# Logsumexp over heads on one core: one more head summed by ScalarE, 80 bias columns moved from GpSimd to VectorE, four more tiles in 4 MB loads

## The chip, the cores and the metric

The kernel runs on one core of a Trainium2 chip. The metric is the device time of one execution in microseconds (us), the median of the runs shown. A profile comes from one profiled execution; its span runs from the first to the last recorded event on the core.

## The reference

```python
B, S, D, H = 8, 2048, 2048, 8          # x: (B, S, D) float32, bias: (H, D // H)
x_heads = x.reshape(B, S, H, Dh).transpose(0, 2, 1, 3)      # Dh = 256
x_heads = x_heads + bias[None, :, None, :]
x_tiled = np.repeat(x_heads, 2, axis=2)
mx = x_tiled.max(axis=-1, keepdims=True)
lse = mx.squeeze(-1) + np.log(np.exp(x_tiled - mx).sum(axis=-1))   # (B, H, 2 * S)
```

For each row of x and each of its eight heads: add the head's 256 biases, take the exponentials, sum them, take the logarithm, and write the result twice. x has 134 MB and is read once; the output has 1 MB. The kernel sums exponentials without taking the maximum off first, watches for sums out of the usual range, and has a second way for that case (`all_again`), which does not run here.

## The kernel before, in words

**Tiles.** A tile t is 256 rows of x: 128 partitions with K = 2 rows each, 2 MB. There are 64 tiles, eight to a batch. SBUF holds eight tiles at a time, as four 4 MB buffers `xb` of two tiles each. `load` (L228, L243) issues all loads of x on SyncE's (SP's) queue: tiles 0 and 1 by themselves, then from tile 2 up to `BLOCKS` - 1 in blocks of 4 MB for two tiles, then tile by tile (2 MB), from tile 57 on by single rows (1 MB), and the last three tiles in an order written out by hand (`TAIL_LOADS`, 1 MB down to 128 KB). A load into a buffer waits until the last readers of the tiles that were in it are done (`last_uses`); `reload` issues it right after the work of the tile that frees it. SP also issues the stores of the results, behind all loads. Each DMA reports to one of eight semaphores in turn, and a DMA waits for the earlier DMA that reported to the same one.

**Three stages** (`STAGES`). Tiles 0 to 53 use `BULK`, called whole tiles below; tiles 54 to 56 use `MIXED`; from tile 57 on rows are done singly, and from tile 61 on the steps follow a list written out by hand (`TAIL`).

**A whole tile** divides its eight heads between engines by the numbers in `BULK`:

- Heads 0 to 2 (`pe=3`): TensorE puts the bias into PSUM (`put_bias`, L370) and adds x to it (`late_heads`, L428). Head 0 lies in the bank `one_ps`, heads 1 and 2 in one of two pairs of banks, `pair`, which alternate. ScalarE takes the exponentials. For head 0 it sums them on the way, once for each of the two rows (`acc=1`, L439: an activation and a read of its accumulator); for heads 1 and 2 it only writes them back to `xb`, 1024 elements in one instruction (L446).
- Head 3 (columns 768 to 1023): ScalarE takes the exponential of x without a bias, and VectorE multiplies by the exponential of the bias, which lies in the PSUM tile `w_ps` (L496).
- Heads 4 to 7 (from `g0=4`, columns 1024 to 2047): GpSimd adds the bias in place (`g_add`, L478), then ScalarE takes the exponential, in the same instruction as that of head 3 (L484, 2560 elements).
- VectorE sums the exponentials of heads 1 to 7, 3584 elements into 14 sums (L503).

The steps L484, L496 and L503 of a tile stand in `later`, which the program issues in the next tile's turn. `MIXED` tiles do without VectorE's late product over head 3: there GpSimd adds the bias to heads 4 to 7, ScalarE sums two heads, and VectorE multiplies and sums two heads (`weigh`, L519).

**Order.** The order of all instructions on each engine is the order in which the program issues them (`manual_schedule`); nothing moves them later.

**At the start**, ScalarE's queue fetches the bias into `brow` (L280). GpSimd splits the first three heads' bias into three bf16 parts (L293 to L297), which ScalarE's queue copies into `b3` (L298); the first two tiles use the parts directly. TensorE spreads the bias over the partitions (L303) for `b_rep` and `w_ps`.

**At the end of a batch**, its sums are turned by TensorE and logged by ScalarE. For batch 6 (tiles 48 to 55) `turn_two` (L713) does the one after tile 59, and `finish_two` (L726) the other after tile 60.

Of the kernel before, what the change touches and what calls it, by code (L numbers as in the profile page):

```python
# [12 lines left out]
ACT = mybir.ActivationFunctionType  # L13
# [3 lines left out]

K = 2
KB = 4
BLOCKS = 42  # L20

NBUF = 8

# [7 lines left out]

BULK = dict(pe=3, acc=1, g0=4, late=True, fold=0)
MIXED = dict(pe=2, acc=2, g0=4, late=False, fold=0)
PROMPT_F1 = dict(pe=2, acc=2, g0=8, late=False, fold=1)
FOLD = 32
# [55 lines left out]
def kernel(  # L93
# [6 lines left out]
    nc = tc.nc  # L100
    P = nc.NUM_PARTITIONS
    B, S, D = x.shape
    H, Dh = bias.shape
# [4 lines left out]
    T = B * NBLK  # L108
# [3 lines left out]
    CPE = BULK["pe"] * Dh  # L112
    MM = 512
# [9 lines left out]
    brow = sb.tile([1, D], F32, name="brow")  # L123
# [5 lines left out]
    b3 = sb.tile([P, CPE], BF16, name="b3")  # L129
    bparts = sb.tile([1, 3, CPE], BF16, name="bparts")  # L130
# [38 lines left out]
    xts = [xb[:, k : k + K] for xb in xbs for k in range(0, KB, K)]  # L169
# [49 lines left out]
    last_uses = [[] for _ in range(T)]  # L219
# [51 lines left out]
    for set_idx, (_name, funcs) in enumerate(get_activation_tables(nc.m.arch).items()):  # L271
        if ACT.Exp in funcs and ACT.Ln in funcs:
# [4 lines left out]
                )  # L277
            )
            break
    nc.scalar.dma_start(  # L280
        out=brow.rearrange("p (h j) -> p h j", h=H), in_=bias.unsqueeze(0)
    )
    for t in range(NBUF):
        load(t)
    nc.vector.memset(ones, 1.0)
# [9 lines left out]
    nc.gpsimd.tensor_copy(bparts[:, 1], brest[:, 0])  # L295
    nc.gpsimd.tensor_sub(brest[:, 1], brest[:, 0], bparts[:, 1])
    nc.gpsimd.tensor_copy(bparts[:, 2], brest[:, 1])  # L297
    nc.scalar.dma_start(out=b3[0:3, :], in_=bparts)  # L298

# [5 lines left out]
    for i, c in enumerate(range(G0, D, MM)):  # L307
        spread(ps[i], c, c + MM)
        nc.vector.tensor_copy(b_rep[:, c - G0 : c - G0 + MM], ps[i])
    W_LATE = BULK["g0"] * Dh  # L310
    w_late = w_ps[:, 0 : W_LATE - W0]
    spread(w_late, W0, W_LATE)
    nc.scalar.activation(out=w_late, in_=w_late, func=ACT.Exp)
# [109 lines left out]
    def late_heads(m, t, got, sums):  # L423


        mms = []
        for h, p in enumerate(got[:-1]):
            mm = nc.tensor.matmul(  # L428
                p,
                lhsT=ident,  # L430
                rhs=xts[t % NBUF][:, :, h * Dh : (h + 1) * Dh],
                start=False,
                stop=True,
            )
            mms.append(on_x(t, mm, [loads[t, 0, 0]]))

        def pe_part():
            for k in range(K):
                act = nc.scalar.activation(  # L439
                    out=xts[t % NBUF][:, k, 0:Dh],  # L440
                    in_=got[0][:, k * Dh : (k + 1) * Dh],
                    func=ACT.Exp,
                    accum_out=sums[:, k, 0:1],
                )
                last_uses[t].append(on_x(t, act, [mms[0]]))
            act = nc.scalar.activation(  # L446
                out=xts[t % NBUF][:, :, Dh : m["pe"] * Dh].rearrange(
                    "p k (h j) -> p h k j", j=Dh
                ),
                in_=got[-1].rearrange("p (h k j) -> p h k j", k=K, j=Dh),  # L450
                func=ACT.Exp,
            )
            on_x(t, act, [mms[-1]])

        return pe_part
# [17 lines left out]
        )  # L473

    def g_add(m, t, k0, k1):
        c = m["g0"] * Dh
        v = xts[t % NBUF][:, k0:k1, c:D]
        add = nc.gpsimd.tensor_tensor(  # L478
            out=v, in0=v, in1=each_row(b_rep, c - G0, D - c, k1 - k0), op=ALU.add
        )  # L480
        return on_x(t, add, [loads[t, k0, 0]])
# [4 lines left out]
    def later(m, t, k0, k1, sums, add):  # L486
# [2 lines left out]
        v = xts[t % NBUF][:, k0:k1, h0 * Dh : D]  # L489
        done = exp_inplace(t, v, add)  # L490
        if m["late"]:
            n = (m["g0"] - h0) * Dh
            f = v[:, :, 0:n]
            h0 = m["acc"]
            v = xts[t % NBUF][:, k0:k1, h0 * Dh : D]
            mul = nc.vector.tensor_tensor(  # L496
                out=f,
                in0=f,
                in1=each_row(w_ps, m["pe"] * Dh - W0, n, k1 - k0),
                op=ALU.mult,  # L500
            )
            done = on_x(t, mul, [done])
# [356 lines left out]
    for t in range(T_TAIL):  # L859
# [71 lines left out]
        for i, (_, b1) in enumerate(groups):  # L931
            if t - 2 == b1 * NBLK - 1:
                finish(i)
                ends_of(i)
        if t == T - 5:
            turn_two()
        if t == T - 4:
            finish_two()
    store()
    last_bank = heads[0][2]  # L940
# [57 lines left out]
```

## Time and profile before

| what | us |
|---|---|
| median of 3 runs | 322.7 (322.33 to 323.44) |
| the profiled execution | 322.41 |
| its span | 320.5 |
| VectorE busy | 286.8 |
| GpSimd busy | 287.2 |
| ScalarE busy | 264.0 |
| TensorE busy | 248.8 |

In the profile, PE is TensorE, PEld its weight loads, DVE is VectorE, ACT is ScalarE, POOL is GpSimd, SP is SyncE. L12 is line 12 of the kernel. A row of a group of instructions has line, engine, operation, output and input tiles with partitions x elements, the count, busy time and mean duration in ns, and then the engine's idle time before them with what ended it. A row by stretches of the span has for each engine its busy time and count, then TensorE's granted clock (1.00 is full), the mean busy share of the 16 DMA engines (a packet is booked at one moment, so single stretches can go over 1) and the GB/s that they moved. Records on one engine overlap a little, so the distance from one start to the next is shorter than a duration.

### The profile page before, as it was taken

How to read it: one execution, taken by the hardware profiler on the slowest of the kernel's cores; microseconds unless marked ns; L12 is line 12 of the kernel's file. 1: busy time of each engine (PE TensorE's matmuls, PEld its weight loads, DVE VectorE, ACT ScalarE, POOL GpSimd, SP SyncE). 2: the span in 40 equal slices, each digit the busy share in tenths (PEclk: the TensorE clock that was granted, in tenths of full speed). 3: DMA queues.
4: the chain of work that ended last, by engine and by line, in shares of the span. 5: the costliest groups of instructions: out<-in, count | busy, mean ns of one | idle time of the engine just before them, and what ended most of it. 6: DMA issues, size and time to landing. Idle time of an engine off the chain costs nothing.

```text
span 320.5 us, 2268 instructions
## 1 busy us (share of the span) xinstructions
PE 248.8 (78%) x610; PEld 99.1 (31%) x610; DVE 286.8 (89%) x307; ACT 264.0 (82%) x434; POOL 287.2 (90%) x118
## 2 busy tenths in 40 slices
PE   5998884877887877869788776688877787678873
PEld 2333331323333323323233322233332332233321
DVE  2347999799969999996999999989999999999995
ACT  1159977888599788878979988879888998999996
POOL 7939997999999999999999989999999999987864
PEclk9979998999598999968989999989999999799999
DMA  7999999999999999999999999999999999999995
GB/s 310 444 425 458 413 439 436 413 454 405 450 450 401 451 423 429 454 405 447 450 406 454 417 431 454 401 431 431 433 433 425 428 431 430 421 429 427 422 415 224
DMA packets 8950, 135.44 MB, mean 423 GB/s; under 512 B 996, under 2 KB 1383, under 8 KB 2791
## 3 DMA queue, kind: packets, MB, share of 16 engines
q1 hardware_dynamic: 8784, 135.14, 98.6%
q10 hardware_dynamic: 152, 0.14, 0.1%
q8 instruction: 5, 0.08, 0.1%
q14 instruction: 9, 0.07, 0.1%
HBM read 134.23 MB, written 1.05 MB: 422 GB/s over the span
## 4 chain that ended last, share of the span: by engine, by line
DMA 49%; ACT 20%; DVE 13%; PE 13%; POOL 4%; issue 0%; SPq 0%
DMA xb<-in_x_dram 48%; ACT xb L484 12%; DVE R L503 11%; PE pair L428 6%; POOL xb L478 4%; PE one_ps L428 3%; ACT xb L459 3%; ACT xb L446 3%; DVE xb L496 2%; PE pair L303 1%; PE pair L370 1%; ACT xb L439 1%; PE one_ps L370 1%; DMA brow<-in_bias_dram 1%; ACT xb L832 0%
## 5 line engine op out<-in xcount | busy, mean ns | idle before, releaser
L478 POOL TENSOR_TENSOR xb<-xb,b_rep 128x2048 f32<-128x2048 f32 x57 | 257.6, 4542 | 19.5 <-DMA xb<-in_x_dram 19.5
L503 DVE TENSOR_REDUCE R<-xb 128x14 f32<-128x3584 f32 (+1 forms) x57 | 216.8, 3803 | 2.1 <-ACT xb L484 0.2
L484 ACT ACTIVATE xb<-xb 128x2560 f32<-128x2560 f32 (+5 forms) x78 | 155.9, 2008 | 17.6 <-POOL xb L478 17.6
L428 PE MATMUL pair<-xb,ident 128*128 128x512 f32 x216 | 111.9, 644 | 0.0
L428 PE MATMUL one_ps<-xb,ident 128*128 128x512 f32 x108 | 62.9, 666 | 17.1 <-DMA xb<-in_x_dram 17.1
L446 ACT ACTIVATE xb<-pair 128x1024 f32<-128x1024 f32 x54 | 55.5, 1028 | 19.8 <-PE pair L428 19.5
L428 PEld LDWEIGHTS pair<-xb,ident 128*128 128x128 f32 x216 | 45.3, 210 | 59.4 <-issue 59.4
L496 DVE TENSOR_TENSOR xb<-xb,w_ps 128x512 f32<-128x512 f32 x54 | 36.7, 680 | 22.0 <-ACT xb L484 22.0
L370 PE MATMUL one_ps<-b,ones_bf 128*128 128x512 bf16 x52 | 20.1, 387 | 36.7 <-ACT xb L439 36.7
L439 ACT ACTIVATE xb<-one_ps 128x256 f32<-128x256 f32 x108 | 39.9, 378 | 6.6 <-PE one_ps L428 6.4
L370 PEld LDWEIGHTS <-ones_bf 128*128 128x128 bf16 (+1 forms) x174 | 17.6, 101 | 85.7 <-issue 78.8
L370 PE MATMUL pair<-b,ones_bf 128*128 128x512 bf16 x104 | 31.1, 380 | 0.0
L428 PEld LDWEIGHTS one_ps<-xb,ident 128*128 128x128 f32 x108 | 19.5, 198 | 32.2 <-DMA xb<-in_x_dram 26.1
L519 DVE CUSTOM_DVE_ANT_0 xb<-xb,w_ps 128x256 f32<-128x256 f32 x61 | 22.3, 418 | 0.1
L439 ACT ACTIVATION_READ_ACCUMULATOR xb<-one_ps 128x1 f32 x108 | 22.1, 205 | 0.0
L405 PE MATMUL pair<-xb,ident 128*128 128x512 f32 x28 | 16.5, 692 | 6.8 <-DMA xb<-in_x_dram 6.8
L542 POOL TENSOR_TENSOR xb<-xb 128x128 f32<-128x128 f32 (+3 forms) x39 | 15.2, 389 | 4.8 <-ACT xb L832 2.0
L459 ACT ACTIVATE xb<-pair 128x256 f32<-128x256 f32 x37 | 14.0, 397 | 0.1
L821 PE MATMUL pair<-xb,ident 128*128 128x512 f32 (+1 forms) x18 | 8.1, 533 | 3.5 <-DMA xb<-in_x_dram 3.4
L536 POOL TENSOR_TENSOR xb<-xb,w_sb 128x256 f32<-128x256 f32 (+1 forms) x10 | 7.8, 783 | 3.1 <-ACT xb L484 2.6
L405 PEld LDWEIGHTS pair<-xb,ident 128*128 128x128 f32 x28 | 4.9, 207 | 14.9 <-DMA xb<-in_x_dram 12.9
L459 ACT ACTIVATION_READ_ACCUMULATOR xb<-pair 128x1 f32 x37 | 8.3, 224 | 0.0
(61 smaller groups left out, 83.2 us busy)
## 6 DMA issues: line engine op xcount, KB each, us to landing
xb<-in_x_dram SPq DMA_DIRECT2D x20, 4096.0 KB, 21.6
xb<-in_x_dram SPq DMA_DIRECT2D x17, 2048.0 KB, 22.2
xb<-in_x_dram SPq DMA_DIRECT2D x10, 1024.0 KB, 22.0
xb<-in_x_dram SPq DMA_DIRECT2D x2, 640.0 KB, 16.2
xb<-in_x_dram SPq DMA_DIRECT2D x4, 256.0 KB, 8.7
xb<-in_x_dram SPq DMA_DIRECT2D x1, 768.0 KB
xb<-in_x_dram SPq DMA_DIRECT2D x2, 384.0 KB, 13.0
out_dram<-res SPq DMA_DIRECT2D x1, 512.0 KB, 5.8
```

The source lines that it names most:

```text
L370: nc.tensor.matmul(p, lhsT=lhsT, rhs=each_row(b, h * Dh, Dh, K), start=i == 0, stop=False,)
L405: mm = nc.tensor.matmul(p, lhsT=ident, rhs=xts[t % NBUF][:, ka:kb, c : c + w], start=False, stop=True,)
L428: mm = nc.tensor.matmul(p, lhsT=ident, rhs=xts[t % NBUF][:, :, h * Dh : (h + 1) * Dh], start=False, stop=True,)
L439: act = nc.scalar.activation(out=xts[t % NBUF][:, k, 0:Dh], in_=got[0][:, k * Dh : (k + 1) * Dh], func=ACT.Exp, accum_out=sums[:, k, 0:1],)
L446: act = nc.scalar.activation(out=xts[t % NBUF][:, :, Dh : m["pe"] * Dh].rearrange("p k (h j) -> p h k j", j=Dh), in_=got[-1].rearrange("p ...
L459: act = nc.scalar.activation(out=xts[t % NBUF][:, k, h * Dh : (h + 1) * Dh], in_=p, func=ACT.Exp, accum_out=sums[:, k, h : h + 1],)
L478: add = nc.gpsimd.tensor_tensor(out=v, in0=v, in1=each_row(b_rep, c - G0, D - c, k1 - k0), op=ALU.add)
L484: return on_x(t, nc.scalar.activation(out=v, in_=v, func=ACT.Exp), [after])
L496: mul = nc.vector.tensor_tensor(out=f, in0=f, in1=each_row(w_ps, m["pe"] * Dh - W0, n, k1 - k0), op=ALU.mult,)
L503: red = nc.vector.tensor_reduce(out=sums[:, k0:k1, h0:H], in_=v.rearrange("p k (h j) -> p k h j", j=Dh), op=ALU.add, axis=mybir.AxisListTy ...
L519: ttr = nc.vector.tensor_tensor_reduce(out=v, in0=v, in1=w, scale=1.0, scalar=0.0, op0=ALU.mult, op1=ALU.add, accum_out=dst,)
L542: done = nc.gpsimd.tensor_tensor(out=v[:, :, 0:n], in0=v[:, :, 0:n], in1=v[:, :, n : 2 * n], op=ALU.add)
```

## The change

Whole tiles are divided otherwise: `acc=2`, so ScalarE sums heads 0 and 1 itself, in four activations, and writes head 2 back with an activation of 512 elements; VectorE's product takes `MORE = 80` columns beyond head 3, GpSimd's addition starts 80 columns later, and VectorE's sum covers heads 2 to 7, 3072 elements. `w_ps` is filled 80 columns further at the start. `BLOCKS` goes from 42 to 46, so tiles 42 to 45 come in two loads of 4 MB instead of four of 2 MB. The bias and its parts are each fetched in two DMAs. The turning and the logarithm of batch 6 come after tiles 57 and 58. With the two DMAs more at the start the semaphores of the DMAs fall otherwise; the fourth 4 MB load then waits for the first load of all.

```diff
-BLOCKS = 42
+BLOCKS = 46
-BULK = dict(pe=3, acc=1, g0=4, late=True, fold=0)
+BULK = dict(pe=3, acc=2, g0=4, late=True, fold=0)
+
+MORE = 80
...
-    nc.scalar.dma_start(
-        out=brow.rearrange("p (h j) -> p h j", h=H), in_=bias.unsqueeze(0)
-    )
+    for h in range(0, H, H // 2):
+        nc.scalar.dma_start(
+            out=brow.rearrange("p (h j) -> p h j", h=H)[:, h : h + H // 2],
+            in_=bias[h : h + H // 2].unsqueeze(0),
+        )
...
-    nc.scalar.dma_start(out=b3[0:3, :], in_=bparts)
+    for c0, c1 in ((0, MM), (MM, CPE)):
+        nc.scalar.dma_start(out=b3[0:3, c0:c1], in_=bparts[:, :, c0:c1])
...
-    W_LATE = BULK["g0"] * Dh
+    W_LATE = BULK["g0"] * Dh + MORE
...
         def pe_part():
-            for k in range(K):
-                act = nc.scalar.activation(
-                    out=xts[t % NBUF][:, k, 0:Dh],
-                    in_=got[0][:, k * Dh : (k + 1) * Dh],
-                    func=ACT.Exp,
-                    accum_out=sums[:, k, 0:1],
-                )
-                last_uses[t].append(on_x(t, act, [mms[0]]))
+            for h in range(m["acc"]):
+                for k in range(K):
+                    act = nc.scalar.activation(
+                        out=xts[t % NBUF][:, k, h * Dh : (h + 1) * Dh],
+                        in_=got[h][:, k * Dh : (k + 1) * Dh],
+                        func=ACT.Exp,
+                        accum_out=sums[:, k, h : h + 1],
+                    )
+                    last_uses[t].append(on_x(t, act, [mms[h]]))
+            h = m["acc"]
             act = nc.scalar.activation(
-                out=xts[t % NBUF][:, :, Dh : m["pe"] * Dh].rearrange(
-                    "p k (h j) -> p h k j", j=Dh
-                ),
-                in_=got[-1].rearrange("p (h k j) -> p h k j", k=K, j=Dh),
+                out=xts[t % NBUF][:, :, h * Dh : m["pe"] * Dh],
+                in_=got[h].rearrange("p (k j) -> p k j", j=Dh),
                 func=ACT.Exp,
             )
...
     def g_add(m, t, k0, k1):
-        c = m["g0"] * Dh
+        c = m["g0"] * Dh + (MORE if m["late"] else 0)
...
         if m["late"]:
-            n = (m["g0"] - h0) * Dh
+            n = (m["g0"] - h0) * Dh + MORE
...
-        if t == T - 5:
+        if t == T - 7:
             turn_two()
-        if t == T - 4:
+        if t == T - 6:
             finish_two()
```

## The prediction

> **What bounds the kernel now.** I read the page from the top: busy shares first, then the DMA queue, then the load stream by stage.
>
> ```profile
> span 320.5 us, 2268 instructions
> PE 248.8 (78%) x610; PEld 99.1 (31%) x610; DVE 286.8 (89%) x307; ACT 264.0 (82%) x434; POOL 287.2 (90%) x118
> ...
> q1 hardware_dynamic: 8784, 135.14, 98.6%
> ```
>
> Two engines stand at 90%, but the queue of loads stands at 98.6% of the span. An average can hide a starved stage, so the next view is the busy time by stretches of the span; its last two columns are the DMA share and the GB/s.
>
> ```profile
> 60.00:100.00 40.00, 31.84 (x77) 12.45 (x76) 36.12 (x17) 34.15 (x54) 37.47 (x9) 0.91 1.00 433
> 204.00:240.00 36.00, 27.41 (x70) 11.47 (x69) 34.56 (x17) 31.14 (x49) 35.40 (x9) 0.95 0.99 425
> 240.00:270.00 30.00, 23.04 (x63) 9.39 (x62) 29.79 (x15) 27.62 (x43) 30.00 (x7) 1.00 1.01 430
> 300.00:310.00 10.00, 7.70 (x23) 3.14 (x22) 9.96 (x61) 10.00 (x26) 6.93 (x16) 1.00 1.01 419
> ```
>
> The DMA share is full in every stage, whichever engine is busiest beside it: the loads follow each other without a hole. The chain of work that ended last, in order of time, says how far the engines are from opening one (start, duration, what):
>
> ```profile
> 31.60 21.45 DMA xb<-in_x_dram
> ...
> 148.91 0.73 ACT xb L439 x4
> 149.64 0.91 ACT xb L446
> 150.55 2.23 ACT xb L484
> ...
> 187.32 20.63 DMA xb<-in_x_dram
> ...
> 224.73 0.60 DVE xb L496
> ...
> 251.88 24.21 DMA xb<-in_x_dram
> ...
> 283.60 1.45 ACT xb L459 x8
> ...
> 304.83 0.48 ACT xb L832
> ```
>
> The load issued at 31.60 is that of tiles 8 and 9 (four 4 MB buffers hold tiles 0 to 7) and lands at 53.05. The one at 187.32 is the last 4 MB load, tiles 40 and 41, and lands at 207.95. They are 16 loads apart: (207.95 - 53.05) / 16 = 9.681 us each, **4.841 us a tile**. The load at 251.88 follows VectorE's sum of tile 47, so it is tile 55; it lands at 276.09, 14 tiles of 2 MB after 207.95: **4.867 us a tile**. A 4 MB load that needs 9.68 us lands 21.45 or 20.63 us after its issue, so about 11 us of other loads stand ahead of it. An engine may release a buffer 11 us later than now before the queue runs dry. That is the cover for nearly everything below.
>
> The end of the span is tied to the same stream:
>
> ```profile
> 300.80 1.13 PE L405 MATMUL pair<-xb,ident 128*128 128x512 f32 x2 [0.44 <-DMA xb<-in_x_dram]
> ...
> 305.68 1.13 PE L821 MATMUL pair<-xb,ident 128*128 128x512 f32 x2 [0.46 <-DMA xb<-in_x_dram]
> ```
>
> ```profile
> 315.69 0.30 PEld L821 LDWEIGHTS pair<-xb,ident 128*128 128x128 f32 x2 [0.67 <-DMA xb<-in_x_dram]
> ```
>
> ```profile
> 302.88 0.58 ACT L726 ACTIVATE res_two<-pair 64x512 f32<-64x512 f32 x1
> 303.36 1.48 ACT L484 ACTIVATE xb<-xb 128x1536 f32<-128x1536 f32 x1
> ...
> 305.65 1.48 ACT L484 ACTIVATE xb<-xb 128x1536 f32<-128x1536 f32 x1
> ...
> 316.57 0.38 ACT L459 ACTIVATE xb<-pair 128x256 f32<-128x256 f32 x1
> ```
>
> TensorE still waits for data at 305.68 and at 315.69. ScalarE has no gap in the tail, but its exponential at 305.65 starts just as the data that TensorE waited for comes in; and its last sum at 316.57 can't be much earlier, since the last matmul, started at 315.69, ends near 316.4. From the last landing to the end of the span it is 320.5 - 315.7 = 4.8 us, and the change touches none of it.
>
> **The change part by part.** The rows that price it, from the groups with shapes kept apart:
>
> ```profile
> L478 POOL TENSOR_TENSOR xb<-xb,b_rep 128x2048 f32<-128x2048 f32 x57 | 257.6, 4542 | 19.5 <-DMA xb<-in_x_dram 19.5
> L503 DVE TENSOR_REDUCE R<-xb 128x14 f32<-128x3584 f32 x54 | 209.9, 3888 | 1.9
> L428 PE MATMUL one_ps<-xb,ident 128*128 128x512 f32 x108 | 62.9, 666 | 17.1 <-DMA xb<-in_x_dram 17.1
> L439 ACT ACTIVATE xb<-one_ps 128x256 f32<-128x256 f32 x108 | 39.9, 378 | 6.6 <-PE one_ps L428 6.4
> L496 DVE TENSOR_TENSOR xb<-xb,w_ps 128x512 f32<-128x512 f32 x54 | 36.7, 680 | 22.0 <-ACT xb L484 22.0
> L439 ACT ACTIVATION_READ_ACCUMULATOR xb<-one_ps 128x1 f32 x108 | 22.1, 205 | 0.0
> L503 DVE TENSOR_REDUCE R<-xb 128x8 f32<-128x2048 f32 x3 | 6.9, 2284 | 0.2 <-ACT xb L484 0.2
> L484 ACT ACTIVATE xb<-xb 128x2048 f32<-128x2048 f32 x3 | 5.8, 1920 | 0.2 <-POOL xb L478 0.2
> ```
>
> *ScalarE, 54 whole tiles.* Before, back to back: two summed heads 0.73, the exponential of 1024 0.91, that of 2560 2.23, together 3.87 us. After: four summed exponentials (eight records, four of them accumulator reads, take 1.45 in the chain row at 283.60), one of 512 elements (0.48, row at 304.83) and 2.23: **4.16 us**, 0.29 more. If neither reads nor starts overlapped it would be 4 x (0.378 + 0.205) + 0.58 (512 elements, row at 302.88) + 2.23 = 5.14. I take 4.16, since the chain shows four of them in a row. It lies under the 4.84 us between tiles.
>
> *VectorE.* The sum shrinks from 3584 to 3072 elements; by (3888 - 2284) / 1536 = 1.04 ns an element that is 0.53 less. The product grows from 512 to 672: 0.17 more. Start to start 4.51 (0.60, 3.89 and the gaps) becomes about **4.15 us**.
>
> *GpSimd.* 1888 instead of 2048 elements. In proportion, 4.54 becomes 4.19. At worst nothing is saved.
>
> So all three stand under 4.84 a tile, before and after. In the bulk that buys a buffer released about 1 us sooner, a longer queue, and no time: the stream is the limit. **0 us**; if GpSimd or VectorE grew instead, the 11 us would cover it.
>
> *4 MB loads for tiles 42 to 45.* Two loads fewer on SP, and four tiles at 4.841 instead of 4.867: **-0.1 us**. The lower end is the whole shortfall of the stretch 204 to 240, 36 x (433 - 425) / 433 = -0.7; the upper end is 0, as the step down from one form to the other remains, only later. Here a rule speaks for more. The Trainium skill, page "DMA: Bandwidth & Descriptors", section "Anatomy of one DMA", puts a transfer at about 2.0 us plus its bytes, so two fewer would be 4.0 us. By that rule the time is 318.4; the trace disagrees, since a pair of 2 MB loads takes 2 x 4.867 - 9.681 = 0.05 us more than one of 4 MB.
>
> *What a later switch costs.* Tile 44 and 45 land together, so the engines start the 2 MB stretch a tile behind. GpSimd's own order of time shows this before:
>
> ```profile
> 208.02 63.11 POOL L478 TENSOR_TENSOR xb<-xb,b_rep 128x2048 f32<-128x2048 f32 x14 [0.60 <-DMA xb<-in_x_dram]
> 271.31 4.55 POOL L478 TENSOR_TENSOR xb<-xb,b_rep 128x2048 f32<-128x2048 f32 x1 [0.18 <-DMA xb<-in_x_dram]
> 276.16 4.54 POOL L478 TENSOR_TENSOR xb<-xb,b_rep 128x2048 f32<-128x2048 f32 x1 [0.30 <-DMA xb<-in_x_dram]
> ```
>
> 14 adds without a wait at 63.11 / 14 = 4.51, then waits for data of 0.18 and 0.30: it catches up just at tile 54. After, it has ten whole tiles (44 to 53) and tile 54, whose add stays at 4.55, until tile 55 lands 10 x 4.867 = 48.67 later. With 4.51 x 1888 / 2048 = 4.16 that is 46.15: caught up with 2.5 us to spare. The limit is 4.41 an add. ScalarE's limit, worked out the same way: until its last exponential of tile 55 (4.6 after the landing, behind GpSimd) it has 48.67 + 4.6 = 53.3 us. From that go a first wait for TensorE (two matmuls, 1.3), and of tiles 54 and 55 eight sums (2.9), two exponentials of 1024 (1.8) and one of 2048 (1.9). The other 45.4 are for ten tiles: 4.54 each, against 4.16. **0 us.** What is late next, tile 55's add at 276.16, hangs on its landing, and from there the order of work is the old one.
>
> *Batch 6 logged two tiles sooner.* Its transposes and its logarithm (0.48, from 302.88 to 303.36) move ahead of the rows of tile 59. ScalarE is then 0.48 later at tiles 59 and 60 and at most 0.15 earlier at the exponential of 303.36, whose data land at 303.2; the next, at 305.65, waits for data anyway. TensorE's transposes need tile 55's sum, which VectorE makes no later than now. SP's stores stay behind the loads. **0 us**, bounds -0.15 and +0.1.
>
> *Bias and its parts in two DMAs each.*
>
> ```profile
> 0.79 0.54 ACTq L280 DMA_DIRECT2D brow<-in_bias_dram  x1
> ...
> 8.50 8.96 POOL L478 TENSOR_TENSOR xb<-xb,b_rep 128x2048 f32<-128x2048 f32 x2
> 8.56 0.82 ACTq L298 DMA_DIRECT2D b<-bparts  x1
> ...
> 14.26 0.38 ACT L439 ACTIVATE xb<-one_ps 128x256 f32<-128x256 f32 x1 [4.46 <-PE one_ps L428]
> ```
>
> The second issues cost ScalarE's queue at most 0.54 and 0.82, and the wider spread of w_ps a little TensorE time. ScalarE idles 4.46 us there, and the first buffer's release at 31.5 could be 11 us later. The semaphores of the DMAs also move round: the fourth 4 MB load now waits until the first load has landed. That landing is before 8.5, where GpSimd starts on it, and 10 MB (about 23 us) are queued by then. **0 us**; without the covers 0.5 to 1.4.
>
> *Sum.* 322.41 (the profiled execution; span 320.5 and 1.9 around it) - 0.1 = 322.3. The runs shown have their median at 322.7, so 322.6 by that one. I take **322.5**.
>
> **The rivals.**
>
> *ScalarE becomes the bound (slower).* It is the only engine that gets more work. Between 4.54 and 4.84 us a tile it enters the tail late by ten times the excess, up to 3.0 us: 325.3; at 5.14 it sets the bulk too and the time goes beyond 335 (54 x 0.3 more, and the end after it). For it: it has no gap in the tail to make lateness good. Against: the row of 1.45 for four sums. Chance 0.09.
>
> *GpSimd's add does not shrink.* Then 10 x 4.51 + 4.55 - 48.67 = 1.0 us late at tile 55, and 0.1 from the loads: 323.3. Against: one shape alone is in the trace, but time that does not go with the elements would be odd. Chance 0.04.
>
> *A load pays more per transfer than its bytes (faster).* With the whole shortfall of 204 to 240 gone: 321.7. For it: 425 against 433. Against: 4.867 a tile over all 14. Chance 0.06; for the price of the rule above, 318.4, chance 0.01.
>
> *The change does nothing at all in the time.* It can't be told from the forecast.
>
> **How the numbers follow.** Forecast 0.80, within 322.0 to 323.1 by itself. A measurement of this kernel tells about 0.3% (1.0 us) from no change. Faster than that: 0.07, all of the third rival. Slower: 0.10, the first rival and a part of the second. Within: 0.83. The range reaches to both near rivals, 321.7 to 323.7.
>
> **What would show it.** Right: the loads' share still near 98.6% and 433 GB/s up to about 227 us; ScalarE's four summed heads at about 1.45 a tile and its busy time up by 15 to 30 us (records overlap); VectorE's sum near 3.35 and product near 0.85; GpSimd's add near 4.19, with waits for data from tile 52 on; TensorE waiting for data up to the last load. Wrong: a DMA share under 0.97 in any stretch of the bulk, GpSimd or ScalarE without a wait up to tile 55, or TensorE in the tail waiting for ScalarE instead of for data.

## The result, and the profile after

The changed kernel takes 323.55 us (median of 22 runs, 323.15 to 324.67), the kernel before 322.64 beside it (22 runs, 322.2 to 323.68): ratio 1.0027, 95% interval 1.0018 to 1.0036. The forecast was 322.5 us and no change that can be told; with this many runs 0.27% slower can be told. The profiled execution of the kernel after took 323.56, its span is 321.7. The executions of the kernel before fall in two groups, 322.1 to 322.9 and 323.0 to 324.1 us, so a median of few runs can lie between them, and the landings in the traces are compared beside the times.

The page of the profile of after, top and DMA queues (a queue's row has packets, MB and the share of 16 engines' span):

```profile
span 321.7 us, 2484 instructions
PE 248.8 (77%) x610; PEld 100.2 (31%) x610; DVE 268.1 (83%) x307; ACT 278.9 (87%) x650; POOL 269.1 (84%) x118
...
q1 hardware_dynamic: 8496, 135.14, 98.3%
...
q8 instruction: 5, 0.08, 0.1%
q14 instruction: 11, 0.09, 0.1%
```

The same page of before has one row that the prediction passed over:

```profile
q14 instruction: 9, 0.07, 0.1%
```

VectorE lost 18.7 us of work, GpSimd 18.1, and ScalarE gained 14.9, as planned. The loads are still the limit, at 98.3%. But there are 216 records more, all on ScalarE (434 to 650), and two more 8 KB packets on the queue q14, over which instructions are fetched.

The groups of after with shapes kept apart show that the sizes came out as forecast:

```profile
L483 POOL TENSOR_TENSOR xb<-xb,b_rep 128x1888 f32<-128x1888 f32 x54 | 225.8, 4205 | 36.9 <-DMA xb<-in_x_dram 32.5 <-DVE R L321 4.4
L508 DVE TENSOR_REDUCE R<-xb 128x12 f32<-128x3072 f32 x54 | 181.1, 3354 | 1.9
L501 DVE TENSOR_TENSOR xb<-xb,w_ps 128x672 f32<-128x672 f32 x54 | 46.1, 853 | 35.3 <-ACT xb L489 35.3
```

Stretches of after (engines as before; the last two columns are DMA share and GB/s):

```profile
60.00:100.00 40.00, 31.31 (x71) 12.41 (x71) 32.80 (x16) 33.82 (x78) 33.68 (x9) 0.87 1.00 433
204.00:240.00 36.00, 28.64 (x64) 11.33 (x63) 29.76 (x15) 31.47 (x76) 31.43 (x8) 0.86 0.99 425
```

By these rows the stream is as dense as before (433 and 425 there as well). The loss shows only where an engine waits for a load. TensorE in order of time, before, then after; the first two rows are tiles 55 and 56:

```profile
276.14 3.50 PE L405 MATMUL pair<-xb,ident 128*128 128x512 f32 x4 [2.43 <-DMA xb<-in_x_dram]
281.02 1.99 PE L405 MATMUL pair<-xb,ident 128*128 128x512 f32 x4 [0.95 <-DMA xb<-in_x_dram]
...
303.23 1.13 PE L821 MATMUL pair<-xb,ident 128*128 128x512 f32 x2 [0.44 <-DMA xb<-in_x_dram]
```

```profile
276.49 1.98 PE L410 MATMUL pair<-xb,ident 128*128 128x512 f32 x4 [2.19 <-DMA xb<-in_x_dram]
282.04 2.85 PE L410 MATMUL pair<-xb,ident 128*128 128x512 f32 x3 [3.13 <-DMA xb<-in_x_dram]
...
304.03 1.12 PE L826 MATMUL pair<-xb,ident 128*128 128x512 f32 x2 [0.49 <-DMA xb<-in_x_dram]
...
316.60 0.70 PE L826 MATMUL pair<-xb,ident 128*128 128x256 f32 x2
```

Before, tile 56 lands 281.02 - 276.14 = 4.88 us behind tile 55. After, it is 282.04 - 276.49 = 5.55: a **step of 0.67 us**. It isn't the only one, since tile 55 is 0.35 late already (276.49 to 276.14). GpSimd in order of time, in after, shows another:

```profile
208.00 8.34 POOL L483 TENSOR_TENSOR xb<-xb,b_rep 128x1888 f32<-128x1888 f32 x2 [1.29 <-DMA xb<-in_x_dram]
217.67 8.39 POOL L483 TENSOR_TENSOR xb<-xb,b_rep 128x1888 f32<-128x1888 f32 x2 [1.33 <-DMA xb<-in_x_dram]
228.01 33.37 POOL L483 TENSOR_TENSOR xb<-xb,b_rep 128x1888 f32<-128x1888 f32 x8 [1.95 <-DMA xb<-in_x_dram]
261.91 4.22 POOL L483 TENSOR_TENSOR xb<-xb,b_rep 128x1888 f32<-128x1888 f32 x1 [0.53 <-DMA xb<-in_x_dram]
```

Two blocks of 4 MB land 217.67 - 208.00 = 9.67 us apart, the next 228.01 - 217.67 = 10.34 later: **0.67 again**. The stream of before has smaller delays of its own, so in the end after is 0.80 later at the first row of the tail (304.03 to 303.23; I call it the tail's first landing below) and 0.91 at the last matmul (316.60 to 315.69). ScalarE's end in after, beside the two rows of before that it answers to (its last sum at 316.57 is in the prediction; this is its last issue):

```profile
317.72 0.45 ACT L464 ACTIVATE xb<-pair 128x256 f32<-128x256 f32 x1
...
319.10 0.39 ACTq L743 DMA_DIRECT2D out_dram<-res_last  x1
```

```profile
317.88 0.39 ACTq L738 DMA_DIRECT2D out_dram<-res_last  x1
```

The last sum follows the last matmul by 1.12 in place of 0.88. So of the 1.22 us between the last issues, 0.91 are the loads and 0.24 ScalarE's. From the issue to the end of the span it is 2.6 in both.

The trace also lists every DMA packet with queue, size and start. A packet of 8 KB on q14 takes 0.31 us, and each of them falls together with one packet of x, of the 16 or more then under way, that takes 0.2 to 0.55 us longer than others of its size. During the stream the fetches on q14 start at (us):

```
before  47.5  110.4  150.9  163.6  248.5  266.1  296.4
after   37.7   97.5  108.0  161.0  163.8  219.7  269.7  276.7  297.8
```

Those near 110, 164, 268 and 297 occur in both. What is left is 47.5, 150.9, 248.5 before (about 100 apart), and 37.7, 97.5, 161.0, 219.7, 276.7 after (about 60 apart). A whole tile has 6 ScalarE records before (two sums with their reads, two more) and 10 after. At 128 records to a fetch and 4.84 us a tile that gives 128 / 6 x 4.84 = 103 us and 128 / 10 x 4.84 = 62 us. The trace's own count agrees: at these moments ScalarE has 51, 177 and 305 records behind it in before, and 51, 180, 311, 434 and 566 in after. So these are **ScalarE's fetches**, three before and five after, and the last two of after, at 219.7 and 276.7, stand just ahead of the two steps. The Trainium skill, page "Perfetto Trace Analysis", section "The 4-stage abstract model", makes an instruction 64 bytes; 128 of them are 8 KB, as the trace has it.

### The profile page after: what moved, and what is told of

Same layout as the page of the kernel before. It is cut to its first block, busy times and chain, and to the rows that moved or that the text cites. A ratio compares the mean times of both kernels' runs of the same rounds, so it can differ in the third digit from the quotient of the medians.

```text
span 321.7 us, 2484 instructions
## 1 busy us (share of the span) xinstructions
PE 248.8 (77%) x610; PEld 100.2 (31%) x610; DVE 268.1 (83%) x307; ACT 278.9 (87%) x650; POOL 269.1 (84%) x118
## 3 DMA queue, kind: packets, MB, share of 16 engines
q1 hardware_dynamic: 8496, 135.14, 98.3%
## 4 chain that ended last, share of the span: by engine, by line
DMA 45%; DVE 24%; ACT 16%; PE 11%; POOL 3%; issue 0%; SPq 0%
DMA xb<-in_x_dram 43%; DVE R L508 19%; ACT xb L489 11%; DVE xb L501 5%; PE pair L433 3%; ACT xb L464 3%; PE one_ps L433 3%; POOL xb L483 3%; DMA brow<-in_bias_dram 2%; PE pair L308 1%; PE pair L375 1%; PE pair L410 1%; ACT xb L445 1%; ACT xb L453 1%; PE one_ps L375 1%
## 5 line engine op out<-in xcount | busy, mean ns | idle before, releaser
L483 POOL TENSOR_TENSOR xb<-xb,b_rep 128x1888 f32<-128x1888 f32 (+1 forms) x57 | 239.4, 4223 | 38.9 <-DMA xb<-in_x_dram 34.5
L508 DVE TENSOR_REDUCE R<-xb 128x12 f32<-128x3072 f32 (+1 forms) x57 | 188.0, 3298 | 4.6 <-ACT xb L489 2.7
L489 ACT ACTIVATE xb<-xb 128x2560 f32<-128x2560 f32 (+5 forms) x78 | 158.6, 2047 | 4.8 <-POOL xb L483 4.7
L501 DVE TENSOR_TENSOR xb<-xb,w_ps 128x672 f32<-128x672 f32 x54 | 46.1, 853 | 35.3 <-ACT xb L489 35.3
L433 PEld LDWEIGHTS pair<-xb,ident 128*128 128x128 f32 x216 | 45.3, 210 | 59.7 <-issue 59.7
L445 ACT ACTIVATE xb<-one_ps 128x256 f32<-128x256 f32 x108 | 42.4, 422 | 11.3 <-PE one_ps L433 11.1
L445 ACT ACTIVATE xb<-pair 128x256 f32<-128x256 f32 x108 | 42.9, 432 | 6.2 <-PE pair L433 6.1
L453 ACT ACTIVATE xb<-pair 128x512 f32<-128x512 f32 x54 | 35.4, 655 | 4.6 <-PE pair L433 4.4
L445 ACT ACTIVATION_READ_ACCUMULATOR xb<-pair 128x1 f32 x108 | 27.4, 257 | 0.0
L445 ACT ACTIVATION_READ_ACCUMULATOR xb<-one_ps 128x1 f32 x108 | 26.4, 248 | 0.0
L464 ACT ACTIVATE xb<-pair 128x256 f32<-128x256 f32 x37 | 14.3, 409 | 1.0 <-PE pair L410 0.8
(63 smaller groups left out, 98.3 us busy)
```

Source lines behind the costliest of these rows:

```text
L433: mm = nc.tensor.matmul(p, lhsT=ident, rhs=xts[t % NBUF][:, :, h * Dh : (h + 1) * Dh], start=False, stop=True,)
L445: act = nc.scalar.activation(out=xts[t % NBUF][:, k, h * Dh : (h + 1) * Dh], in_=got[h][:, k * Dh : (k + 1) * Dh], func=ACT.Exp, accum_out ...
L453: act = nc.scalar.activation(out=xts[t % NBUF][:, :, h * Dh : m["pe"] * Dh], in_=got[h].rearrange("p (k j) -> p k j", j=Dh), func=ACT.Exp,)
L464: act = nc.scalar.activation(out=xts[t % NBUF][:, k, h * Dh : (h + 1) * Dh], in_=p, func=ACT.Exp, accum_out=sums[:, k, h : h + 1],)
L483: add = nc.gpsimd.tensor_tensor(out=v, in0=v, in1=each_row(b_rep, c - G0, D - c, k1 - k0), op=ALU.add)
L489: return on_x(t, nc.scalar.activation(out=v, in_=v, func=ACT.Exp), [after])
```

## The experiments

Theory at first (called instruction theory in the expectations): the extra records are fetched by the DMA engines that carry the loads, and the stream falls behind at each fetch. Rivals: ScalarE's added time, the bias and the earlier logarithm, the 4 MB loads. Four kernels beside 322.4 us (18 runs of before):

**e1, the two summed heads alone.** Before, with

```diff
-BULK = dict(pe=3, acc=1, g0=4, late=True, fold=0)
+BULK = dict(pe=3, acc=2, g0=4, late=True, fold=0)
...
+            for h in range(m["acc"]):
+                for k in range(K):
...
```

> The kernel before with one part of the change alone: ScalarE sums two heads (108 activations and 108 accumulator reads more), VectorE's sum covers six heads. Four theories of the 0.9 us by which the changed kernel is slower. Instruction theory: the extra ScalarE instructions are fetched by the DMA engines that also load x (the queue of instruction packets carries 11 packets in the changed kernel, 9 before), each fetch holds up one of the 16, and the stream is as late as its slowest: +0.6 to +1.0 us, with 11 instruction packets. ScalarE theory: ScalarE's longer work itself delays the end: +0.6 to +1.0 too. Bias theory (the second half of the bias lands at 6.8 instead of 2.5 us, so all work starts 4 us later): 0. Block theory (4 MB loads for tiles 42 to 45): 0.

323.41 us, ratio 1.0039 (1.0026 to 1.0052), 11 packets on q14:

```profile
276.66 1.98 PE L405 MATMUL pair<-xb,ident 128*128 128x512 f32 x4 [2.44 <-DMA xb<-in_x_dram]
282.21 2.08 PE L405 MATMUL pair<-xb,ident 128*128 128x512 f32 x2 [3.14 <-DMA xb<-in_x_dram]
```

The whole loss is in this part, and the same step (5.55) with it. GpSimd's add and the loads are those of before; VectorE's sum covers one head less, as in after.

**e2, the bias in two DMAs and the logarithm sooner.** Before, with

```diff
+    for h in range(0, H, H // 2):
+        nc.scalar.dma_start(...)
...
-        if t == T - 5:
+        if t == T - 7:
             turn_two()
-        if t == T - 4:
+        if t == T - 6:
             finish_two()
```

> The kernel before with the two small parts of the change: the bias and its parts in two DMAs each, batch 6 logged two tiles sooner. Bias theory: +0.6 to +1.0 us. Instruction, ScalarE and block theory: within 0.2 us of before, with 9 instruction packets.

322.7 us, ratio 1.0014 (1.0004 to 1.0025). The tail's first landing is at 303.26 (0.03 later than before) and the last issue at 317.92 (0.04):

```profile
317.92 0.39 ACTq L743 DMA_DIRECT2D out_dram<-res_last  x1
```

From there to the end of its span of 320.9 it is 3.0 in place of 2.6. So these parts cost nothing up to the last issue. The 0.3 to 0.4 us stand behind it, and in after they are absent.

**e3, the change without the longer run of 4 MB loads.** After, with

```diff
-BLOCKS = 46
+BLOCKS = 42
```

> The changed kernel with 4 MB loads only up to tile 41, as before. Block theory: back to the time before. Instruction, ScalarE and bias theory: as slow as the changed kernel, or 0.1 us slower still: +0.8 to +1.1 us against before.

323.77 us, ratio 1.0045 (1.0032 to 1.0058). Its last matmul of x starts at 316.79, after's at 316.60. The difference of 0.19 can't be put down to the 4 MB loads to tile 45: GpSimd starts on tile 40 at 208.13 here and at 208.00 in after, so 0.13 of it is there before the first load that differs. Here too 3.0 us follow the last issue.

**e4, more ScalarE records that do nothing.** Before, with

```diff
+    spare = sb.tile([P, 256], F32, name="spare")
...
+                if 2 <= t < 45:
+                    for _ in range(5):
+                        nc.scalar.activation(out=spare[0:1, 0:1], in_=ones[0:1, 0:1], func=ACT.Exp)
```

> The kernel before with 215 ScalarE activations of a single element more, five in each of the tiles 2 to 44, which nothing reads: as many instructions as the change adds, no other work. They cost ScalarE some 0.1 to 0.2 us each, in a stage where a tile has about 1 us to spare. Instruction theory: +0.6 to +1.0 us, 11 instruction packets, and the landings fall behind those of the kernel before by steps. ScalarE theory: the same or more, but only if ScalarE comes late into the tail. Bias and block theory: 0.

327.46 us, ratio 1.0166 (1.0153 to 1.0179), 11 packets on q14, tile 56 at 282.07. The step is there, but each of these activations takes 199 ns, so ScalarE was the bound as well and came some 4 us late into the tail. It didn't part the theories.

Next, four kernels beside 322.37 us (26 runs of before):

**e5, more ScalarE time in few records.** Before, with

```diff
+    spare = sb.tile([P, 256], F32, name="spare")
...
+                if m["late"] and t >= 2:
+                    nc.scalar.activation(out=spare, in_=b_rep[:, 0:256], func=ACT.Exp)
```

> The kernel before, with one more ScalarE activation of 256 columns a whole tile (52 in all, about 0.3 us each, as much ScalarE time as the change adds, in 52 records in place of 216). ScalarE theory (its extra time is what delays the loads): +0.9 us, tile 56's data at 282.1 as after. Instruction theory: the 52 records are a quarter of the change's 216, so none or one more 8 KB fetch in the row of the instruction queue (9 or 10 packets), 0 to +0.5 us, tile 56's data at 281.0 to 281.5.

322.79 us, ratio 1.0018 (1.0005 to 1.0032):

```profile
280.92 1.98 PE L406 MATMUL pair<-xb,ident 128*128 128x512 f32 x4 [0.84 <-DMA xb<-in_x_dram]
...
303.59 1.12 PE L822 MATMUL pair<-xb,ident 128*128 128x512 f32 x2 [0.44 <-DMA xb<-in_x_dram]
```

No step up to tile 56, 0.36 at the tail's first landing. Of ScalarE's fetches there are now four in the stream (43.8, 133.9, 218.6, 291.9), the fourth behind tile 56. So ScalarE's time isn't what delays the loads.

**g1, fewer ScalarE records.** Before, without head 0's sums in whole tiles:

```diff
-            for k in range(K):
-                act = nc.scalar.activation(... accum_out=sums[:, k, 0:1])
+            act = nc.scalar.activation(
+                out=xts[t % NBUF][:, :, 0:Dh],
+                in_=got[0].rearrange("p (k j) -> p k j", j=Dh), func=ACT.Exp)
...
```

> The kernel before, with head 0 of the whole tiles exponentiated by one plain activation in place of two that sum (162 ScalarE records fewer; the sums of head 0 are left out). Instruction theory: one or two 8 KB fetches fewer (7 or 8 packets), last data earlier by 0.3 to 0.9 us, the time 321.5 to 322.1 beside 322.4. ScalarE theory: ScalarE is spared 0.9 us a tile that bounds nothing in the kernel before, so no difference. Block theory: no difference.

322.84 us, ratio 1.0014 (1.0002 to 1.0027). Two fetches of ScalarE's in place of three, but the tail's first landing is at 303.14, only 0.09 sooner, and the time isn't better: the instruction theory in its plain form, so much for each fetch, fails below three. The reports of the loads, further down, show why.

**g2, after with still more ScalarE records.** After, with 132 activations of one element in tiles 2 to 54 (two or three a tile, written as in e4).

> The kernel after, with 132 more ScalarE activations of one element, two or three a whole tile in tiles 2 to 54. Instruction theory: one or two more 8 KB fetches than after (12 or 13 packets), last data later by 0.3 to 0.9 us than after's, the time 323.8 to 324.4. ScalarE theory: 0.4 to 0.6 us more ScalarE time a tile on after's 4.16 stays below 4.84 us a tile, so no difference to after, or a little less than e1's whole step.

325.67 us, ratio 1.0096 (1.0082 to 1.011), six fetches of ScalarE's, and the tail's first landing goes on to 304.64. The rest of the time is ScalarE's, whose last sum comes at 319.36, 2.15 behind the last matmul of x.

**h1, after with the bias and the logarithm as before.**

> The kernel after, with the bias in one DMA each and batch 6's log back at tiles T-5 and T-4. Instruction theory: the fetches and the last data as after (11 packets, 316.6). Log theory (the earlier log costs the end 0.2 us, since its ScalarE work falls where tile 56 arrives): last ScalarE sum 0.9 after the data in place of 1.12, the time 323.3. Bias theory (the late bias costs nothing): no difference from it. End theory (two DMAs fewer than after shift which queue comes last, as in e2 and e3): 0.4 us more after the last issue, the time 323.7 at most.

323.55 us, ratio 1.0039 (1.0025 to 1.0053): the time of after. Tile 56 at 282.34, the tail's first landing at 304.30, and the last sum still 1.25 behind the last matmul of x. So the earlier logarithm isn't the cause of after's 1.12 either.

Four kernels beside 322.63 us (29 runs of before):

**i1, the change with fewer ScalarE records.** After, with g1's edit of head 0.

> The kernel after with head 0 of the whole tiles exponentiated by one plain activation in place of two that sum (head 0's sums are left out), so about 2322 records in place of 2484, everything else of the change kept. Fetch theory (the two more instruction fetches put the slowest DMA engine behind): 9 packets in the row of the instruction queue, tile 56's data at 281.0 and the last data at 315.5 to 315.7 (before 315.69, after 316.60), the time 322.2 to 322.5. If the loss came from the 4 MB loads, from the earlier log or from GpSimd's and VectorE's new sizes: the time stays at 323.4.

322.82 us, ratio 1.0006 (0.9992 to 1.0019), four fetches of ScalarE's in place of five:

```profile
280.88 3.32 PE L412 MATMUL pair<-xb,ident 128*128 128x512 f32 x4 [2.48 <-DMA xb<-in_x_dram]
...
303.38 1.12 PE L834 MATMUL pair<-xb,ident 128*128 128x512 f32 x2 [0.44 <-DMA xb<-in_x_dram]
```

The step at tile 56 is gone, with the 80 columns, the bias, the logarithm and the 4 MB loads all as in after.

**i2, the same number of records without the sums.** g1 with seven activations of one element a whole tile.

> The kernel before with head 0 of the whole tiles not summed (as in the run without head 0's sum, which took 322.84 with its lower half at 322.2 to 322.5) and seven ScalarE activations of one element a whole tile: the records of after (about 2481), with ScalarE's time at some 4.4 us a tile or less, below the 4.84 us of a load. Fetch theory: 11 packets, tile 56's data at 282.0 to 282.3, last data at 316.6 to 316.8, the time 323.3 to 323.6. If what counts is the sums or the data that ScalarE and VectorE move, and not the number of records: 322.3 to 322.8.

345.61 us, ratio 1.0709 (1.069 to 1.0727). Seven times 200 ns made ScalarE the bound:

```profile
PE 236.0 (69%) x608; PEld 99.2 (29%) x610; DVE 291.5 (85%) x311; ACT 313.7 (91%) x650; POOL 286.8 (83%) x118
```

I had estimated 4.4 us a tile; the groups of this run add up to 2.32 + 1.00 + 0.57 + 1.40 = 5.29. It tells nothing of the records.

**f1, before with 4 MB loads to tile 43** (`BLOCKS = 44`).

> The kernel before with its 4 MB loads to tile 43 in place of 41 and nothing else. From the -0.19 us that four more tiles in 4 MB loads gave between the runs with 42 and with 46: -0.1 us, 322.25 beside 322.35, as long as GpSimd's 4.54 us an add is done in time for the freed buffers; if it is not, a load's issue waits and the time is up to 0.5 us longer.

322.61 us, ratio 1.0008 (0.9994 to 1.0023), the tail's first landing at 303.09 (0.14 sooner than before). It doesn't last: the last matmul of x starts 0.10 later than before's (315.79 to 315.69), and behind the last issue stand 3.3 us in place of 2.6. So no gain from these loads can be told here either.

**f2, two sums and 80 columns only from tile 38 on.** `BLOCKS = 46`, bias and logarithm as before, and a stage of its own in `STAGES`:

```diff
+LATER = dict(pe=3, acc=2, more=80, g0=4, late=True, fold=0)
...
+    (38, (LATER,)),
...
```

> The kernel after with the two summed heads and the 80 columns only from tile 38 on (one summed head and no columns moved before), the bias in one DMA each and the log at its place before: 32 ScalarE activations more than before in place of 108, some 64 records. Fetch theory: 9 or 10 packets; with 9 the last data at 315.5 (before's 315.69 less the 0.19 of the longer run of 4 MB loads), the time 322.2, which would beat both; with 10 between that and 323.2.

322.92 us, ratio 1.0007 (0.9997 to 1.0017), four fetches of ScalarE's, the tail's first landing at 303.52. No better version than before came out.

So far every kernel changed ScalarE's own instructions. Two more beside 322.49 us (22 runs of before) put the records elsewhere:

**j1, as many records on TensorE.** Before, with

```diff
+                    for _ in range(2):
+                        nc.tensor.matmul(
+                            tp[:, 0, 0:1], lhsT=ones_bf, rhs=ones_bf[:, 0:1], start=True, stop=True
+                        )
```

> The kernel before, with two TensorE matmuls of one column a whole tile that nobody reads (108 matmuls and 108 weight loads, 216 records more: the number that the change adds on ScalarE), ScalarE untouched. Fetch theory (records of any engine are fetched by the DMA engines that carry the loads): 11 packets in the row of the instruction queue, tile 56's data at 281.7 to 282.3 in place of 281.02, last data at 316.3 to 316.8 in place of 315.69, the time 323.0 to 323.6 beside 322.4. If it is ScalarE's sums or its time that put the loads behind: tile 56 at 281.0, last data at 315.7, the time as before, 322.4 to 322.7.

322.39 us, ratio 0.9997 (0.9985 to 1.0008):

```profile
303.15 1.12 PE L821 MATMUL pair<-xb,ident 128*128 128x512 f32 x2 [0.45 <-DMA xb<-in_x_dram]
```

```profile
q8 instruction: 6, 0.10, 0.1%
q14 instruction: 9, 0.07, 0.1%
```

The 216 records are fetched on another queue, q8, in packets of 16 KB: five of them in the stream in place of four, and no landing is late. The theory that records of any engine cost the same falls.

**j2, after with fewer records on TensorE.** After without the matmuls that put the bias of heads 1 and 2 into PSUM.

```diff
+                if h and n_ps[0] > NEARLY:
+                    continue
...
-                start=False,
+                start=h > 0 and t >= NEARLY,
...
```

> The kernel after without the TensorE matmuls that put the bias of heads 1 and 2 into the pair's banks in whole tiles from the third on (the bias of these heads is left out; 104 matmuls and 104 weight loads fewer, about 2276 records), ScalarE, VectorE, GpSimd and the loads as in after. Fetch theory: 9 packets, tile 56's data at 281.0 to 281.3, last data at 315.5 to 315.9, the time 322.2 to 322.8. If ScalarE's four sums, the 80 columns, the earlier log or the longer run of 4 MB loads cost the 0.9 us: tile 56 at 282.0, the time 323.4 to 323.6.

323.34 us, ratio 1.0021 (1.0009 to 1.0034), 11 packets on q14, tile 56 at 282.00, the tail's first landing at 303.98. 208 records fewer on TensorE bring nothing back.

Last, two beside 322.48 us (16 runs of before), to tell records of ScalarE from its sums, and from records of another engine on q14:

**k1, as many records on VectorE.** Before, with four memsets of one element a whole tile.

> The kernel before, with four VectorE memsets of one element a whole tile (216 records more, on VectorE, about 0.2 us of its time a tile). If any 8 KB fetch puts the stream behind: 11 packets in the row of queue q14, tile 56's data at 281.7 to 282.3, the time 323.0 to 323.6 beside 322.4. If only ScalarE's fetches do, always on the same slow DMA engine: 11 packets, tile 56's data at 281.0, last data at 315.7, the time 322.3 to 322.7, as with TensorE's 216.

331.13 us, ratio 1.0265 (1.0249 to 1.0281). 11 packets on q14 and tile 56 at 282.03, but in SP's queue VectorE's added memsets had become the longest wait:

```profile
SPq L229 <- DVE spare L927: 180.1, 17, 27.7
```

The time tells nothing of the fetches, since VectorE was late for the tail; what the landings tell follows below.

**k2, ScalarE records without sums, ScalarE not the bound.** Before, with three activations of one element a whole tile.

> The kernel before, with three ScalarE activations of one element a whole tile (162 records more, ScalarE at some 4.5 us a tile and so not the bound, unlike the run with five a tile). ScalarE-record theory: 10 or 11 packets in the row of q14, tile 56's data at 281.4 to 282.2, last data at 316.1 to 316.8, the time 322.8 to 323.5. If it is the sums and not the records: 281.0, 315.7 and 322.4.

323.36 us, ratio 1.0032 (1.0017 to 1.0047): the loss of the change, with none of its work. ScalarE's fetches are at 37.8, 107.3, 174.4, 241.1 and 302.4. One step sits behind the last of them:

```profile
301.16 1.12 PE L406 MATMUL pair<-xb,ident 128*128 128x512 f32 x2 [0.45 <-DMA xb<-in_x_dram]
...
304.30 1.12 PE L822 MATMUL pair<-xb,ident 128*128 128x512 f32 x2 [1.15 <-DMA xb<-in_x_dram]
```

From 301.16 to 304.30 it is 3.14, where before has 303.23 - 300.80 = 2.43: 0.71 us for one fetch at 302.4. In after the fetch at 276.7 put the same step at tile 56.

The runs that have the landing, sorted by ScalarE's fetches during the stream:

| ScalarE's fetches | tail's first landing (us) |
|---|---|
| 2 | g1 303.14 |
| 3 | before 303.23, e2 303.26, f1 303.09, j1 303.15 |
| 4 | e5 303.59, i1 303.38, f2 303.52 |
| 5 | after 304.03, e1 304.20, e3 304.22, h1 304.30, j2 303.98, k2 304.30 |
| 6 | g2 304.64 |

From three on it is about 0.45 us a fetch.

**Where a fetch strikes.** Each load of x reports sixteen times to its semaphore, as often as there are DMA engines; it has landed with the last report. The trace keeps the time of every report. At the tail's first landing the first report comes at 301.12 to 301.32 us in every kernel here, apart from i2, which ScalarE bounds. So most of each load is on time everywhere. What differs is how far the last report is behind the first: 1.86 us in before, 2.71 in after. It grows at ScalarE's fetches (last report behind the first, in us, for the load before a fetch and the load after it):

| fetch | load before it | load after it |
|---|---|---|
| before, third, 248.5 | 1.63 | 1.90 |
| e5, fourth, 291.9 | 1.81 | 2.50 |
| i1, fourth, 289.6 | 1.61 | 2.17 |
| after, fourth, 219.7 | 1.66 | 2.32 |
| after, fifth, 276.7 | 2.17 | 2.83 |
| k2, fifth, 302.4 | 2.32 | 3.02 |
| g2, sixth, 278.0 | 2.79 | 3.47 |

From the fourth fetch on, each one moves the last report alone, by 0.56 to 0.70 us, in all eleven kernels that have four or more; the other fifteen stay within 0.17 us. A fifth fetch strikes the part of the load that the fourth has made the last one, and g2's sixth strikes it again. So ScalarE's fetches hit the same sixteenth of the loads and add up. Up to the third, the last report belongs to another part, and the delay is hidden behind it: that is why g1's two fetches land no sooner than before's three.

TensorE's fetches hit another sixteenth each time. At the tail's first landing the parts more than 1.3 us behind the first are five in j2, six in before and seven in j1, with three, four and five fetches of TensorE's before it, so theirs don't add up. The first of them isn't free: in after, with TensorE's first fetch at 52.5, the last report goes from 0.72 to 1.85 us behind the first. VectorE's fetches count as well: in k1 the last report falls back from 1.81 to 2.30 and from 2.10 to 3.06 us behind fetches at 158.5 and 261.9, where VectorE has 179 and 307 records behind it.

## Why the prediction was wrong, step by step

**The failed step** is "So all three stand under 4.84 a tile, before and after. In the bulk that buys a buffer released about 1 us sooner, a longer queue, and no time: the stream is the limit. **0 us**". The sizes under it were right. The stream was taken to be the same whatever the engines do as long as they are in time. It isn't, since their instructions come over the same DMA engines: ScalarE's 108 more activations and 108 more accumulator reads come to it as two more fetches, and the last matmul of x came 1.09 us later with this part alone (e1, 316.78 to 315.69). A term of about +1.0 us is missing from the sum. That two fetches would be added could have been worked out from the page of before, which has the 9 packets and ScalarE's 434 records. What they cost no row of before told. The prediction's signs of being wrong didn't show it either: the DMA share stays at 1.00 and 0.99 in the two stretches above, because fifteen sixteenths of each load are on time.

Shown: the loss goes with ScalarE's number of records (e1, k2 bring it, i1 takes it away), not with its time (e5), nor with the sums (k2), TensorE's records (j1, j2), the bias and the logarithm (h1), or the loads (e3). Shown by the reports: a load is there when the last of its sixteen parts is, and from the fourth fetch on ScalarE's put the last part back by 0.56 to 0.70 us each. The fetch's packet of 0.31 us and the packet of x that takes some 0.25 longer beside it make 0.56 of that. Not settled: why ScalarE's fetches always hit the same part, where the rest of up to 0.14 comes from, and why a late part catches up a little between fetches (2.32 to 2.17 us in after). Which DMA engine serves a packet isn't recorded.

**ScalarE.** Forecast: 1.45 for the four sums, 4.16 a tile. ScalarE of after in order of time, one tile without a wait:

```profile
97.84 2.33 ACT L489 ACTIVATE xb<-xb 128x2560 f32<-128x2560 f32 x1
100.06 0.38 ACT L445 ACTIVATE xb<-one_ps 128x256 f32<-128x256 f32 x1
...
101.49 0.62 ACT L453 ACTIVATE xb<-pair 128x512 f32<-128x512 f32 x1
101.97 2.37 ACT L489 ACTIVATE xb<-xb 128x2560 f32<-128x2560 f32 x1
```

The sums take 101.49 - 100.06 = 1.43, the tile 101.97 - 97.84 = 4.13. (The prediction's "two summed heads 0.73" are the two rows of head 0; its sum is right.) Busy time rose by 14.9, just under the 15 to 30 given. The first rival, ScalarE as the bound, didn't come true: the bulk lost nothing but the steps.

**VectorE and GpSimd.** Product 0.853 (forecast 0.85), sum 3.354 (3.35), add 4.205 (4.19). GpSimd waits for each block up to tile 44, runs tiles 44 to 51 without a wait (the row at 228.01) and waits for data again from tile 52 (261.91) to 56, as said, so the second rival fell.

**4 MB loads.** Forecast -0.1. The runs can't tell it from nothing: of the 0.19 from e3 to after 0.13 is there before the first load that differs, and f1 gains nothing by its last matmul. The third rival's -0.7 was too much. The Trainium skill, page "DMA: Bandwidth & Descriptors", section "Anatomy of one DMA", gives about 2.0 us of fixed cost for a transfer that GpSimd issues; the loads here are SP's, and by e3 two transfers fewer gain 0.19 us at most.

**What a later switch costs.** 0 us, right: at tile 54 GpSimd waits 0.67 us for the data in place of 0.18.

**Batch 6 sooner.** 0 us up to the last issue, right by e2 and h1. The 0.24 that ScalarE's last sum is late in after came with neither e1 (0.84 behind its last matmul) nor e3 (0.89), and h1 has it without the earlier logarithm. What it hangs on isn't settled.

**Bias in two DMAs.** 0 us, right for the wrong price. The bound was 0.54 and 0.82; the second half of the bias came 4.3 us later, and the whole start with it. (The 4 MB load that waits for the first load is the third, tiles 6 and 7, not the fourth.) TensorE's first rows, before, then after:

```profile
2.63 2.04 PE L303 MATMUL pair<-brow,ones 1*128 1x512 f32 x2 [2.63 <-DMA brow<-in_bias_dram]
```

```profile
6.95 2.04 PE L308 MATMUL pair<-brow,ones 1*128 1x512 f32 x2 [6.95 <-DMA brow<-in_bias_dram]
```

The 11 us of queued loads covered even that: e2's first landing of the tail is that of before within 0.03.

## What to carry to other kernels

In a kernel that its loads bound, an engine with time to spare isn't free: count the records that an edit adds, as a summing activation is two, and read the rows of the instruction queues beside the queue of loads. Here each fetch of 128 ScalarE records put one sixteenth of the loads back. That cost nothing while another part was later still, and 0.56 to 0.70 us a fetch from the fourth on, more than the change could gain. Look for such a loss as steps in the landings, at rows where an engine waits for data, and compare the first with the last report of a load, since a DMA share of 0.99 to 1.01 and the GB/s of a stretch don't show 0.7 us.

## What the runs showed of the hardware that was not expected

- One 8 KB fetch of 0.31 us moved the landings behind it by 0.67 us (after, twice) and 0.71 us (k2). ScalarE's fetches hit the same one of a load's sixteen parts each time and add up; TensorE's, of 16 KB, hit another part each time, so that one more of them (j1) moved nothing.
- The time from the last issue to the end of the span differs between programs with another number of DMAs, whose eight semaphores fall otherwise. It is 2.6 us in before, after, e1, j1 and k2 (64 DMAs), 3.0 in e2 and e3 (66), 3.3 in f1 (63) and 2.8 in f2 and h1 (62). But g2, with 64, has 3.2, so the number alone doesn't decide it. SP's last wait grows with it; why isn't settled. Waits of SP's queue in before, then in f1:

```profile
SPq L993 <- DMA out_dram<-res_last: 0.4, 1, 0.4
```

```profile
SPq L993 <- DMA out_dram<-res_last: 1.1, 1, 1.1
```

- A ScalarE activation of one element takes about 0.2 us (199 ns in e4, 200 in i2), so it is no cheap filler.
- The profiled execution of j1 took 323.49 us, 1.1 more than its median, with its loads on time. TensorE's granted clock is lowered in its very tail (0.88 in place of 1.00). The stretch of before, then of j1:

```profile
306.00:320.00 14.00, 8.09 (x30) 3.23 (x28) 11.09 (x66) 11.43 (x32) 8.31 (x17) 1.00 0.81 319
```

```profile
306.00:320.00 14.00, 9.19 (x29) 4.07 (x28) 11.14 (x66) 11.59 (x32) 8.04 (x17) 0.88 0.78 310
```

In j1 that goes with 1.2 us of span (its last issue is at 319.09, before's at 317.88), more than the whole effect studied here, so landings were compared rather than single spans.
